# Softmax sums in a two-layer attention kernel: reciprocals of six of eight heads (or pairs of heads) go through DRAM instead of through TensorE

## The chip, the cores and the metric

The kernel runs on one core of a Trainium2 chip. The metric is the device time of one execution in microseconds (us). The core has a matrix engine (TensorE, PE in the profile), three engines for elementwise work (VectorE as DVE, ScalarE as ACT, GpSimd as POOL), and SyncE (SP), which in this kernel does nothing but issue transfers (DMAs). Each engine works through its own list of instructions in order; an instruction that waits holds up everything behind it on that engine. Data on the chip lies in 128 partitions; PSUM holds eight banks for the results of matmuls.

## The reference

A two-layer encoder on 512 frames of 1024 features. Layer one is multi-head latent attention with 8 heads of 128 values; layer two is chunked attention with a learned bias and 16 heads of 64 values. Each is followed by a SwiGLU feed-forward block, and each sub-layer has a norm before and after it. What the change touches is the softmax, the same in both layers:

```python
s = jnp.where(mask[None, None], s, -jnp.inf)
p = jax.nn.softmax(s, axis=-1).astype(v.dtype)
return jnp.einsum('bhqk,bkhd->bqhd', p, v)
```

The kernel computes exp(s) first, multiplies it by the values, and divides by the sum of the exponentials afterwards.

## The kernel before

All activations lie transposed: features on the partitions, the 512 frames along the row. To keep float32 precision with fast matmuls, each operand is split into a high and a low part (`split`, L143: ACT casts to the high part, DVE subtracts it to get the low part), and a product is three matmuls (`mm3`, L354 to L356), or two where one operand is already stacked.

`attention` (L511) runs both attention layers. Time is cut into slots: slot i computes the scores of head i // 4 for the 128 queries of block i % 4. In `scores` (L486) PE writes the scores into a bank of the kind "s" (two of them), DVE adds the mask or bias and finds the extreme value (L492), and ACT takes exp and sums each row into `sums` (L494). Two slots later `turn` (L498) transposes the exponentials on PE into a bank of the kind "t" (two of them, L506), and ACT and DVE split them. When the four blocks of a head are done, its `pv` multiplies by the values: in layer one inside `start_a`, in layer two inside `start_b` (L1502, L1503). `pv` also takes the reciprocals of the sums (L995, L1511) and returns a function `rest` that scales the head's output and splits it into `oh` and `ol`, the operands of the output projection. In between, `weave` puts in matmuls of a filler: the projections that make the queries and keys of later heads (`fill_a`, `fill_b`), and the first half of the output projection.

The sums come out with one query per partition, but the outputs have queries along the row. So the reciprocals have to be turned and spread over all partitions. Before, PE does it. In layer one `spread` (L463) broadcasts each of four columns to 128x128 and transposes it into a "t" bank called `bc` (L467, four PE instructions per head). In layer two two heads share 128 partitions, so the work is done once per pair: ACT writes the eight columns out to a 128x512 tile `rw` (L1514, two copies), and PE transposes that in four pieces into a "t" bank called `rs` (L1523). DVE then multiplies `of`, the output, by that bank (L1000, L1524).

Transfers on SP's list around this work: weight tiles `raw` (L285), the rows of the rotary queries `qr` of layer one (L894), and in layer two the queries and keys of each pair (L1477, twelve transfers per pair, from tiles `fh` and `f`) and one `bias` tile per head (L1454).

A scheduler places the instructions of each engine by its own estimate of when operands are ready and by the order in which the code issues them. So the place of a row on an engine follows from the code only roughly.

Of the kernel before, what the change touches and what calls it, by code (L numbers as in the profile page):

```python
# [10 lines left out]
F32 = mybir.dt.float32  # L11
# [19 lines left out]
NQT = S // P  # L31
# [37 lines left out]
def trunk(ctx: ExitStack, tc: tile.TileContext, a, out):  # L69
# [25 lines left out]
    def small(name="sm"):  # L95
        return sp.tile([P, 4], F32, tag="small", name=name_(name))
# [54 lines left out]
    class Pair:  # L151
# [4 lines left out]
        def __init__(self, src):  # L156
            self.src, self.raw = src, {}
# [313 lines left out]
    def spread_sb(col):  # L471
# [2 lines left out]
        nc.scalar.copy(o, b)  # L474
        return o


    class Head:

        def __init__(self, qk, bt, scale, pv, sums):
            self.qk, self.bt, self.scale, self.pv, self.sums = qk, bt, scale, pv, sums
            self.p, self.pt = {}, None

        def scores(self, qt):  # L486
# [24 lines left out]
    def attention(n_heads, start, fill, first, units, after):  # L511
# [33 lines left out]
        if late:  # L545
            late.pop()()


    class Post:
# [424 lines left out]
    def start_a(h):  # L974
        fill.until(h)
        qh, ql, kh, kl = qk_a.pop(h)
        r = qr.pop(h)

        def qk(o, qt, n):
            q_ = slice(qt * P, (qt + 1) * P)  # L980
            nc.tensor.matmul(o, qh[:, q_], kh[:, :n], start=True, stop=False)
            nc.tensor.matmul(o, qh[:, q_], kl[:, :n], start=False, stop=False)
            nc.tensor.matmul(o, ql[:, q_], kh[:, :n], start=False, stop=False)
            nc.tensor.matmul(o, r[:, q_], kr1[:, :n], start=False, stop=False)
            nc.tensor.matmul(o, r[:, q_], kr2[:, :n], start=False, stop=True)

        def pv(pth, ptl):
            fill.until("v")
            o = bank()
            v_ = slice(h * VD, (h + 1) * VD)  # L990
            for kt in range(NQT):
                q_ = slice(kt * P, S)
                mm3(o[:, q_], (va[kt][:, 0, v_], va[kt][:, 1, v_]), (pth[:, kt, q_], ptl[:, kt, q_]),
                    kt == 0, kt == NQT - 1)
            V.reciprocal(sums, sums)  # L995
            of = U(name="of")
            nc.scalar.copy(of, o)

            def rest():
                V.tensor_tensor(of, of, spread(sums), op=OP.mult)  # L1000
# [7 lines left out]
        return Head(qk, lambda n: mask[:, S - n:], lambda qt: nsq[:, qt:qt + 1], pv, sums)  # L1008

    firsts = []  # L1010
    fill = Filler(fill_a())
    attention(H_A, start_a, fill, 13, 8 + 5 * 7 + 6 + 14, False)
    fill.drain()
    st.close()

# [466 lines left out]
    def start_b(h):  # L1482
# [14 lines left out]
        def pv(pth, ptl):  # L1497
# [11 lines left out]
            V.tensor_tensor(of[(LO, HI)[e]], o[:64], t[:64], op=OP.add)  # L1509
            if e:  # L1510
                V.reciprocal(sums[pr], sums[pr])  # L1511
                rw = U(name="rw")
                for j in range(2):
                    nc.scalar.copy(rw.rearrange("p (i e d) -> p i e d", e=2, d=HD)[:, :, j],  # L1514
                                   sums[pr][:, j].unsqueeze(2).to_broadcast([P, NQT, HD]))

            def rest():
                if e == 0:
                    return
                r = bank("t", "rs")  # L1520
                for i in range(NQT):
                    i_ = slice(i * P, (i + 1) * P)
                    nc.tensor.transpose(r[:, i_], rw[:, i_], ident)  # L1523
# [7 lines left out]
        return Head(qk, lambda n: bt[:, :n][:, ::-1], lambda qt: -1.0, pv, sums[pr][:, e])  # L1531

    bias(0)
    firsts = []
# [13 lines left out]
    for tt in range(NQT):  # L1548
        v_split(b[tt], 1, tt)

    attention(H_B, start_b, fill, 12, 7 * 16 + 14, True)
    fill.drain()
    st.close()

# [89 lines left out]
```

## Time and profile before

| what | us |
|---|---|
| median of 3 runs (lowest to highest) | 1136.78 (1135.42 to 1137.72) |
| the profiled execution | 1136.21 |
| its span in the trace | 1134.4 |
| start and projections, 0 to 60 | 60 |
| attention of layer one, 60 to 165 | 105, PE busy 104.27, DVE 70.58, ACT 62.35 |
| feed-forward of layer one, 165 to 490 | 325, PE busy 321.27, DVE 291.58 |
| shared values, first queries and keys, 490 to 596 | 106, PE busy 104.54 |
| attention of layer two, 596 to 757 | 161, PE busy 158.40, DVE 118.57, ACT 105.35 |
| the rest of layer two, 757 to 1134.4 | 377.4, PE busy 364.72 |

Times inside the trace count from the start of the span. A busy share of PE says less than it seems: matmuls are pipelined, so one that is recorded as 272 ns long lets the next one start after about 110 ns. "Loading weights" on PE (PEld) is the step that puts the stationary operand in place; a wait of PE shows there first.

### The profile page before, as it was taken

What the parts mean: (1) busy time and instruction counts of PE and PEld (TensorE: products, weight loads), DVE (VectorE), ACT (ScalarE), POOL (GpSimd) and SP (SyncE); (2) the same over time, 40 slices, a digit from 0 to 9 for tenths busy, and PEclk for the clock granted to TensorE, in tenths of its full rate; (3) what the DMA queues carried; (4) which work ended last, traced back from release to release, by engine and by line L of the source; (5) the groups of instructions that cost most, each with busy time, mean ns of one, the idle gap of its engine ahead of it and who ended that gap; (6) DMA issues with size and microseconds to landing.
All of it is one profiled execution on the core that took longest, in us unless ns stands there. A gap on an engine that the chain in (4) does not pass through costs nothing.

```text
span 1134.4 us, 18987 instructions
## 1 busy us (share of the span) xinstructions
PE 1109.6 (98%) x6973; PEld 984.5 (87%) x6973; DVE 935.2 (82%) x1675; ACT 682.6 (60%) x1335; POOL 65.1 (6%) x90
## 2 busy tenths in 40 slices
PE   8999999999999999999999999999999999999996
PEld 6888889999999998787888888779999999997785
DVE  7787738999899889879758887648999899889867
ACT  6476637655555556578437766656755555567574
POOL 1200000100000002400000000001000000003300
PEclk9999999999999999999999999999999999999998
DMA  7433125423323349932456656634323422359902
GB/s 234 113 106 94 56 91 188 140 85 93 119 87 97 136 149 261 213 102 70 165 147 167 158 161 154 160 106 170 135 75 93 131 94 100 116 180 260 201 1 75
DMA packets 62414, 149.80 MB, mean 132 GB/s; under 512 B 8368, under 2 KB 10160, under 8 KB 62320
## 3 DMA queue, kind: packets, MB, share of 16 engines
q1 hardware_dynamic: 55840, 137.00, 38.5%
q0 software_dynamic: 6336, 11.54, 6.0%
q8 instruction: 55, 0.90, 0.3%
q14 instruction: 39, 0.32, 0.1%
q10 hardware_dynamic: 144, 0.04, 0.0%
HBM read 119.52 MB, written 8.59 MB: 113 GB/s over the span
## 4 chain that ended last, share of the span: by engine, by line
PE 85%; DVE 7%; ACT 3%; DMA 2%; issue 2%; POOL 1%; SPq 0%; DVEq 0%; POOLq 0%; ACTq 0%
PE al L1378 16%; PE b L354 11%; PE b L355 10%; PE b L356 10%; PE be L1378 8%; PE al L1171 8%; PE ga L1378 4%; PE be L1171 4%; PE de L1171 3%; PE ga L1171 3%; PE pt L506 2%; DVE wlo L145 2%; DMA raw<-in_w_pair 1%; ACT whi L144 1%; PE b L1502 1%
## 5 line engine op out<-in xcount | busy, mean ns | idle before, releaser
L144 ACT CAST whi<-raw 128x1024 fp32r<-128x1024 f32 (+3 forms) x224 | 225.6, 1007 | 213.9 <-PE al L1378 73.1
L145 DVE TENSOR_TENSOR wlo<-raw,whi 128x1024 fp32r<-128x1024 f32 (+3 forms) x224 | 261.0, 1167 | 67.4 <-ACT whi L144 64.9
L1378 PE MATMUL al<-th,whi 128*128 128x256 f32 x432 | 123.2, 285 | 1.8 <-DVE ut L1390 1.8
L1378 PE MATMUL al<-th,wlo 128*128 128x256 f32 x432 | 121.2, 281 | 0.0
L1378 PE MATMUL al<-tl,whi 128*128 128x256 f32 x432 | 121.2, 281 | 0.0
L354 PE MATMUL b<-xh,whi 128*128 128x512 f32 (+1 forms) x304 | 115.7, 383 | 1.8 <-ACT xh L148 1.8
L355 PE MATMUL b<-xl,whi 128*128 128x512 f32 (+1 forms) x304 | 112.9, 371 | 0.0
L356 PE MATMUL b<-xh,wlo 128*128 128x512 f32 (+1 forms) x304 | 112.8, 371 | 0.0
L174 DVE TENSOR_TENSOR raw<-raw,raw 128x1024 f32<-128x1024 f32 x72 | 86.8, 1220 | 3.3 <-DMA raw<-in_w_pair 3.1
L1378 PEld LDWEIGHTS al<-th,whi 128*128 128x128 f32 x432 | 81.4, 188 | 4.1 <-DVE ut L1390 2.2
L1378 PEld LDWEIGHTS al<-th,wlo 128*128 128x128 f32 x432 | 81.4, 188 | 0.0
L1378 PEld LDWEIGHTS al<-tl,whi 128*128 128x128 f32 x432 | 81.4, 188 | 0.0
L494 ACT ACTIVATE p<-p,mn 128x128 f32<-128x128 f32 (+1 forms) x96 | 53.9, 562 | 31.7 <-DVE mn L492 31.5
L145 DVE TENSOR_TENSOR ptl<-pt,pth 128x128 fp32r<-128x128 f32 (+1 forms) x96 | 46.2, 486 | 28.8 <-ACT pth L144 23.2
L354 PEld LDWEIGHTS b<-xh,whi 128*128 128x128 f32 x304 | 57.3, 189 | 9.6 <-ACT xh L148 2.7
L356 PEld LDWEIGHTS b<-xh,wlo 128*128 128x128 f32 x304 | 57.4, 189 | 8.8
L144 ACT CAST whi<-wd 128x512 fp32r<-128x512 f32 x86 | 49.8, 620 | 24.2 <-PE de L1171 8.7
L355 PEld LDWEIGHTS b<-xl,whi 128*128 128x128 f32 x304 | 57.5, 189 | 7.2 <-DVE xl L149 0.5
L145 DVE TENSOR_TENSOR wlo<-wd,whi 128x512 fp32r<-128x512 f32 x86 | 56.4, 686 | 7.6 <-ACT whi L144 7.2
L144 ACT CAST pth<-pt 128x128 fp32r<-128x128 f32 (+1 forms) x96 | 40.3, 424 | 28.6 <-PE pt L506 27.9
L1171 PE MATMUL al<-whi,ph 128*128 128x512 f32 x132 | 51.6, 391 | 0.0
L1171 PE MATMUL al<-whi,pl 128*128 128x512 f32 x132 | 51.6, 391 | 0.0
(304 smaller groups left out, 3260.7 us busy)
## 6 DMA issues: line engine op xcount, KB each, us to landing
raw<-in_w_pair SPq DMA_DIRECT2D x72, 512.0 KB, 3.6
wd<-in_w_down SPq DMA_DIRECT2D x54, 256.0 KB, 5.6
raw<-in_w_o SPq DMA_DIRECT2D x16, 512.0 KB, 3.5
raw<-in_w_gu SPq DMA_DIRECT2D x16, 512.0 KB, 3.8
raw<-in_w_down SPq DMA_DIRECT2D x16, 512.0 KB, 4.5
raw<-in_w_qkb SPq DMA_DIRECT2D x16, 512.0 KB, 3.5
wd<-in_w_down POOLq DMA_DIRECT2D x22, 256.0 KB, 5.4
wd<-raw POOLq DMA_DIRECT2D x22, 256.0 KB, 5.3
```

Source lines behind the costliest of these rows:

```text
L144: return (nc.scalar.copy(dst_hi, src), V.tensor_tensor(dst_lo, src, dst_hi.bitcast(F32), op=OP.subtract))
L145: V.tensor_tensor(dst_lo, src, dst_hi.bitcast(F32), op=OP.subtract))
L174: V.tensor_tensor(t, x, y, op=OP.add)
L354: nc.tensor.matmul(o, l[0], r[0], start=start, stop=False)
L355: nc.tensor.matmul(o, l[0], r[1], start=False, stop=False)
L356: nc.tensor.matmul(o, l[1], r[0], start=False, stop=stop)
L494: nc.scalar.activation(p[:, :n], p[:, :n], AF.Exp, bias=mn[:, :1], scale=-1.0, accum_out=self.sums[:, qt:qt + 1])
L506: nc.tensor.transpose(t[:, kt * P:(kt + 1) * P], p[:, kt * P:(kt + 1) * P], ident)
L1171: nc.tensor.matmul(to[e], l[c], r[d], start=j < 4 and k == 0 and n == 0, stop=k == NF // 2 - 1 and n == 2, skip_group_check=True)
L1378: nc.tensor.matmul(o, l[c], r[d], start=first_ and n == 0, stop=k == K2 - 1 and n == 2, skip_group_check=True)
L1502: nc.tensor.matmul(o[:, q_], vv, pth[:, kt, q_], start=kt == 0, stop=False)
```

## The change

For the first six of the eight heads of layer one, and the first six of the eight pairs of layer two, the reciprocals no longer pass through PE. A new function `spread_far` writes them to a small DRAM tensor `sums` in the order of the queries (one transfer per head, so two for a pair; the 128x4 tile goes out as 512 separate elements of four bytes), and reads that row of 2 KB back once for every partition into a tile `bc` of 128x512 (one transfer of 256 KB for a head of layer one, two of 128 KB for a pair). All of them are issued by SP; the reading transfer waits until the writing one has landed. The multiplication on DVE then reads `bc` instead of a PSUM bank. `attention` no longer runs `rest` at the next slot (layer one) or in the same group of slots (layer two), but four slots after `pv` for the far heads and one slot after for the last two (`near`), which keep the way through PE.

```diff
+    def spread_far(sums, n, to):
+        row = a["sums"][to]
+        for e in range(n):
+            v = sums[:, e] if n > 1 else sums
+            nc.sync.dma_start(row[e].rearrange("(t p) -> p t", p=P), v)
+        o = U(name="bc")
+        w = P // n
+        for e in range(n):
+            nc.sync.dma_start(o[e * w:e * w + w], bass.AP(tensor=row.tensor, offset=row[e].offset, ap=[[0, w], [1, S]]))
+        return o
...
@@ attention
-            if late and not after:
-                late.pop()()
             if i >= 6 and i % NQT == 2:
                 t = heads.pop((i - 6) // NQT)
-                late.append(t.pv(*t.pt))
+                rest = t.pv(*t.pt)
+                late.append((i + (1 if t.near else NQT), rest))
             if 2 <= i < slots + 2:
                 t, qt = divmod(i - 2, NQT)
                 heads[t].turn(qt)
-            if late and i % NQT == 3:
-                late.pop()()
+            while late and i >= late[0][0]:
+                late.pop(0)[1]()
...
@@ pv of layer one
+            far = None if near else spread_far(sums, 1, h)
 
             def rest():
-                V.tensor_tensor(of, of, spread(sums), op=OP.mult)
+                V.tensor_tensor(of, of, spread(sums) if near else far, op=OP.mult)
...
-        sums = small("sums")
+        sums, near = small("sums"), h >= H_A - 2
...
@@ pv of layer two
             if e:
                 V.reciprocal(sums[pr], sums[pr])
-                rw = U(name="rw")
-                for j in range(2):
+                rw = U(name="rw") if near else spread_far(sums[pr], 2, H_A + pr)
+                for j in range(2 if near else 0):
                     nc.scalar.copy(rw.rearrange("p (i e d) -> p i e d", e=2, d=HD)[:, :, j],
                                    sums[pr][:, j].unsqueeze(2).to_broadcast([P, NQT, HD]))
 
             def rest():
                 if e == 0:
                     return
-                r = bank("t", "rs")
-                for i in range(NQT):
+                r = bank("t", "rs") if near else rw
+                for i in range(NQT if near else 0):
                     i_ = slice(i * P, (i + 1) * P)
                     nc.tensor.transpose(r[:, i_], rw[:, i_], ident)
                 V.tensor_tensor(of, of, r, op=OP.mult)
...
+        near = pr >= H_B // 2 - 2
...
+    aps["sums"] = nc.dram_tensor("sums", (H_A + H_B // 2, 2, S), F32, kind="Internal").ap()
```

What this does to the lists of three engines is shown at three places. In the rows of the changed kernel the line numbers are its own: L354 to L356 and L145 are unmoved, L506 has become L519, L492 L505, L1494 L1507, L1495 L1508, L1477 L1490, L1454 L1467, and L1000 L1013.

First PE in layer two, at the scaling of the second pair; `sc` are scores, `pt` the transposed exponentials, `b` a projection of the filler. Before:

```order
L506 MATMUL pt_7248<-ident,p_7182 128x128 x2
L354 MATMUL b_7175<-xh_6122,whi_7099 128x512
L355 MATMUL b_7175<-xl_6123,whi_7099 128x512
L356 MATMUL b_7175<-xh_6122,wlo_7100 128x512
L1494 MATMUL sc_7269<-k_2_6796,q_2_6795 128x128
L1523 MATMUL rs_7253<-ident,rw_7219 128x128 x4
L1495 MATMUL sc_7269<-k_2_6797,q_2_6795 128x128
```

The same place in the changed kernel:

```order
L519 MATMUL pt_7235<-ident,p_7167 128x128 x2
L354 MATMUL b_7160<-xh_6110,whi_7079 128x512
L355 MATMUL b_7160<-xl_6111,whi_7079 128x512
L356 MATMUL b_7160<-xh_6110,wlo_7080 128x512
L1507 MATMUL sc_7246<-k_2_6784,q_2_6783 128x128
L1508 MATMUL sc_7246<-k_2_6785,q_2_6783 128x128
```

The four transposes into `rs` are gone and nothing has come in their place on PE; that is so at all twelve places.

Second SP in layer two, from the bias tile after the keys of pair 2 to the first keys of pair 3. Before:

```order
L1454 DMA bias_7266<-in_rel 128x512
L1477 DMA q_3_7056<-fh_7167 64x512 x2
L1477 DMA q_3_7056<-f_7166 64x512 x2
L285 DMA raw_7758<-in_w_qkb 128x1024
L1454 DMA bias_7376<-in_rel 128x512
L1477 DMA k_3_7057<-fh_7296 64x512 x2
```

In the changed kernel:

```order
L1467 DMA bias_7243<-in_rel 128x512
L483 DMA sums<-sums_6917 128x4x1 x2
L1490 DMA q_3_7036<-fh_7152 64x512
L1490 DMA q_3_7036<-f_7151 64x512
L1490 DMA q_3_7036<-fh_7152 64x512
L1490 DMA q_3_7036<-f_7151 64x512
L285 DMA raw_7729<-in_w_qkb 128x1024
L487 DMA bc_7206<-sums 64x512 x2
L1467 DMA bias_7358<-in_rel 128x512
L1490 DMA k_3_7037<-fh_7273 64x512 x2
```

The two writes of pair 1 stand ahead of the queries of pair 3, the two reads ahead of the next bias tile and of the keys of pair 3.

Third DVE in layer one, where the second half of the rotary queries has just been made and the scores of head 3's last block (128x512) and of head 4's first (128x128) are handled; `ql` and `kl` are the low parts of queries and keys of heads 4 and 5. Before:

```order
L492 ISA p_1238,mn_1239<-sc_1232,mask,nsq 128x512
L492 ISA mn_1239 128x1
L145 TENSOR_TENSOR ol_1252<-of_1214,oh_1251 128x512
L145 TENSOR_TENSOR ptl_1217<-pt_1255,pth_1216 128x2x128
L995 RECIPROCAL sums_1099<-sums_1099 128x4
L145 TENSOR_TENSOR ptl_1217<-pt_1277,pth_1216 128x3x128
L145 TENSOR_TENSOR ql_1223<-b_1157,qh_1222 128x512
L145 TENSOR_TENSOR ptl_1217<-pt_1305,pth_1216 128x4x128
L145 TENSOR_TENSOR kl_1225<-b_1228,kh_1224 128x512
L145 TENSOR_TENSOR wlo_1533<-raw_1296,whi_1532 128x1024
L145 TENSOR_TENSOR ql_1313<-b_1273,qh_1312 128x512
L492 ISA p_1269,mn_1270<-sc_1263,mask,nsq 128x128
```

In the changed kernel:

```order
L145 TENSOR_TENSOR ptl_1211<-pt_1266,pth_1210 128x3x128
L145 TENSOR_TENSOR wlo_1518<-raw_1285,whi_1517 128x1024
L145 TENSOR_TENSOR ql_1222<-b_1148,qh_1221 128x512
L145 TENSOR_TENSOR kl_1224<-b_1227,kh_1223 128x512
L145 TENSOR_TENSOR ql_1302<-b_1262,qh_1301 128x512
L145 TENSOR_TENSOR kl_1304<-b_1307,kh_1303 128x512
L145 TENSOR_TENSOR ol_1218<-of_1053,oh_1217 128x512
L505 ISA p_1237,mn_1238<-sc_1231,mask,nsq 128x512
L505 ISA mn_1238 128x1
L505 ISA p_1258,mn_1259<-sc_1252,mask,nsq 128x128
L505 ISA mn_1259 128x1
L1013 TENSOR_TENSOR of_1205<-of_1205,bc_1208 128x512
```

The last scores of head 3, which stood ahead of the low parts of the queries and keys, now stand behind all four of them. Behind the scores follows the scaling of head 2, whose tile `bc` SP reads only after the sixteen `qr` transfers.

More of the change, by code (lines that the diff above doesn't have):

```diff
@@ L509, in turn, with attention @@
             split(self.pt[0][:, :qt + 1, q_], self.pt[1][:, :qt + 1, q_], tv)
-    def attention(n_heads, start, fill, first, units, after):
+    def attention(n_heads, start, fill, first, units):
         slots = n_heads * NQT
@@ L541, in attention @@
                 heads[t].turn(qt)
[L542 to L543 removed]
+            while late and i >= late[0][0]:
+                late.pop(0)[1]()
             weave(first + rate * (i + 1))
[L545 to L546 removed]
+        while late:
+            late.pop(0)[1]()
     class Post:
@@ L1005, in pv @@
             return rest
-        sums = small("sums")
-        return Head(qk, lambda n: mask[:, S - n:], lambda qt: nsq[:, qt:qt + 1], pv, sums)
+        sums, near = small("sums"), h >= H_A - 2
+        return Head(qk, lambda n: mask[:, S - n:], lambda qt: nsq[:, qt:qt + 1], pv, sums, near)
     firsts = []
     fill = Filler(fill_a())
-    attention(H_A, start_a, fill, 13, 8 + 5 * 7 + 6 + 14, False)
+    attention(H_A, start_a, fill, 13, 8 + 5 * 7 + 6 + 14)
     fill.drain()
@@ L1529, in pv @@
             return rest
-        return Head(qk, lambda n: bt[:, :n][:, ::-1], lambda qt: -1.0, pv, sums[pr][:, e])
+        near = pr >= H_B // 2 - 2
+        return Head(qk, lambda n: bt[:, :n][:, ::-1], lambda qt: -1.0, pv, sums[pr][:, e], near)
     bias(0)
@@ L1549, in trunk @@
         v_split(b[tt], 1, tt)
-    attention(H_B, start_b, fill, 12, 7 * 16 + 14, True)
+    attention(H_B, start_b, fill, 12, 7 * 16 + 14)
     fill.drain()
```

4 lines of the change are left out of this document (2 added, 2 removed).

## The prediction

> **What bounds the kernel now.** I read the page first: busy times, the slices, and the chain of work that ended last.
>
> ```profile
> span 1134.4 us, 18987 instructions
> PE 1109.6 (98%) x6973; PEld 984.5 (87%) x6973; DVE 935.2 (82%) x1675; ACT 682.6 (60%) x1335; POOL 65.1 (6%) x90
> PE   8999999999999999999999999999999999999996
> PE 85%; DVE 7%; ACT 3%; DMA 2%; issue 2%; POOL 1%; SPq 0%; DVEq 0%; POOLq 0%; ACTq 0%
> ```
>
> PE is busy nearly everywhere and makes up 85% of the chain; transfers make up 2%. So an instruction taken from PE should shorten the time, as long as PE really is what the stage waits for. The change touches the two attention stages only, so I read those in stretches of 20 us (columns: length, then busy us and instructions of PE, PEld, DVE, ACT, POOL, PE clock, DMA share, GB/s).
>
> ```profile
> 80.00:100.00 20.00, 19.77 (x116) 17.01 (x116) 14.91 (x35) 10.97 (x29) 0.00 (x0) 1.00 0.10 34
> 100.00:120.00 20.00, 19.64 (x118) 16.78 (x117) 16.27 (x41) 14.72 (x37) 0.00 (x0) 1.00 0.43 126
> 620.00:640.00 20.00, 19.89 (x113) 16.52 (x112) 18.38 (x43) 14.89 (x38) 0.29 (x2) 1.00 0.63 165
> 640.00:660.00 20.00, 19.87 (x113) 16.62 (x112) 18.20 (x44) 14.82 (x38) 0.29 (x2) 1.00 0.63 154
> 720.00:740.00 20.00, 18.85 (x97) 14.18 (x96) 14.22 (x37) 13.04 (x33) 0.00 (x0) 1.00 0.52 131
> ```
>
> In layer one DVE has 4 to 5 us of 20 free, in layer two at first under 2. PE bounds both, but in layer two DVE is close behind, and towards its end (720 to 740) PE itself waits 1.2 us of 20.
>
> **What PE is relieved of.** The chain, in order of time (start, length, what), shows what a group of four transposes holds up:
>
> ```profile
> 81.39 0.44 PE bc L467 x4
> 134.80 0.44 PE bc L467 x4
> 638.57 0.66 PE rs L1523 x4
> 715.82 0.44 PE rs L1523 x4
> ```
>
> One transpose is recorded as 274 ns (row below), but four take 0.44 us of the chain, since they overlap; the 0.66 counts the last one to its end. Twelve groups go: 12 x 0.44 = **5.3 us**. With them go waits. The groups by line (busy us, mean ns, then idle before and its releasers):
>
> ```profile
> L467 PE MATMUL bc<-ident,sums 128*128 128x128 f32 x32 | 4.8, 274 | 0.0
> L1523 PEld LDWEIGHTS rs<-ident,rw 128*128 128x128 f32 x32 | 3.4, 141 | 3.0 <-ACT rw L1514 1.5 <-issue 0.6 <-DVE ptl L145 0.5
> ```
>
> In layer one PE did not wait ahead of `bc`. In layer two its weight loading waited 3.0 us ahead of eight `rs` groups, 2.3 us for six. What stands behind them on PE are transposes of exponentials, which wait for the same ACT and the same "t" banks, so part of that wait will only move. Between 0 and 2.3 I take the middle, **1.1 us**.
>
> The other removed and changed instructions:
>
> ```profile
> L1514 ACT COPY rw<-sums x16: 390/402/406, 619.7 to 757.1; 128x256 f32<-128x256 f32 x16
> L1000 DVE TENSOR_TENSOR of<-of,bc x8: 675/682/689, 81.9 to 165.1; 128x512 f32<-128x512 f32 x8
> L145 DVE TENSOR_TENSOR ol<-of,oh 128x512 fp32r<-128x512 f32 x8 | 5.5, 690 | 1.4 <-ACT oh L144 1.3
> ```
>
> Twelve copies of 0.40 us leave ACT, which has 5 us of 20 free: no gain beyond the wait just counted. The multiplication reads SBUF in place of PSUM: `of<-of,bc` from PSUM takes 682 ns, `ol<-of,oh` from SBUF 690, so nothing changes on DVE.
>
> **What SP gets.** Per layer-one head one write and one read, per pair two and two. No transfer of this trace moves 512 pieces of four bytes. The nearest rows (KB each, median us to landing; then the timeline of SP and the issue times in ns):
>
> ```profile
> rot<-sincos SPq DMA_DIRECT2D x4, 48.0 KB, 1.7
> inv<-in_inv_freq SPq DMA_DIRECT2D x1, 0.5 KB, 2.7
> bias<-in_rel SPq DMA_DIRECT2D x16, 256.0 KB, 3.3
> k<-fh SPq DMA_DIRECT2D x32, 128.0 KB, 2.4
> 34.63 1.76 SPq L818 DMA_DIRECT2D rot<-sincos  x4
> L1477 SPq DMA_DIRECT2D k<-fh x32: 461/591/603, 569.6 to 730.0; - x32
> L1454 SPq DMA_DIRECT2D bias<-in_rel x16: 328/334/529, 503.1 to 714.1; - x16
> ```
>
> A small write to DRAM (`rot`) lands after 1.7 us. `inv` is 128 pieces of four bytes, a read, and lands after 2.7; if all of that grew with the number of pieces, 512 would take 10.8. So a write lands between 1.7 and 10.8 us; I take 2.7, the row with the same kind of piece (with 1.7 fixed and 1.0 for each 128 pieces it would be 5.7). The reads are the size of `bias` (3.3) and `k` (2.4). Issuing takes 1.76 / 4 = 0.44 us each, as `rot` does; 64 rows of `k` take longer than 128 of `bias`, so issue time does not follow the number of pieces.
>
> Can SP hold that in layer two? The reciprocals of pairs 1 and 2, and SP's transfers between them:
>
> ```profile
> 632.41 0.18 DVE L1511 RECIPROCAL sums<-sums 128x8 f32<-128x8 f32 x1
> 633.54 1.10 SPq L1477 DMA_DIRECT2D q<-fh  x2
> 638.34 0.33 SPq L1454 DMA_DIRECT2D bias<-in_rel  x1
> 644.08 1.11 SPq L1477 DMA_DIRECT2D k<-fh  x2
> 648.74 0.20 DVE L1511 RECIPROCAL sums<-sums 128x8 f32<-128x8 f32 x1 [0.55 <-ACT p L494]
> ```
>
> A pair lasts 16.3 us. SP is busy for 12 x 0.59 with queries and keys, and about 1.4 with two bias and two weight tiles (0.33 each, up to 0.4 with gaps): 8.5 us. Four new issues make 1.8, and 6.0 are left for waiting. The writes go out at about 632.7 and 633.1, ahead of q, which then is done at about 636.2; the second has landed at 636.2 by my value, so the reads go out at 636.7 and 637.1, and land by 640.4 even at 3.3. Behind the waiting read stand the bias tile, which SP issued at 638.34, and the keys at 644.08: neither is late. The multiplication stands some twenty instructions behind the reciprocal on DVE's list, which is nearly full there, so it comes after about 643. So for most pairs the new waits cost nothing; where a write stands behind eight key transfers (8 x 0.6 = 4.8 us, pairs 3 and 5) it may be late. I put 0 in the sum and keep 0 to 2 us.
>
> **A place that gets worse.** In layer one around 100 us the lists are rearranged (third place in the change). The timeline there, before:
>
> ```profile
> 102.62 0.48 DVE L492 CUSTOM_DVE_ANT_0 p<-sc,mask,nsq 128x256 f32<-128x256 f32 x1
> 104.64 0.75 DVE L492 CUSTOM_DVE_ANT_0 p<-sc,mask,nsq 128x512 f32<-128x512 f32 x1 [0.19 <-PE sc L985]
> 107.64 1.22 SPq L894 DMA_DIRECT2D qr<-rl  x2
> 108.44 0.39 PE L356 MATMUL b<-ckh,wlo 128*128 128x512 f32 x1
> 109.72 1.23 DVE L145 TENSOR_TENSOR wlo<-raw,whi 128x1024 fp32r<-128x1024 f32 x1 [0.34 <-ACT whi L144]
> 110.75 0.28 PE L985 MATMUL sc<-kr,qr 128*128 128x256 f32 x1
> ```
>
> Before, the 128x512 scores left their bank at 105.4 (104.64 + 0.75), and PE ended head 4's 128x256 scores at 111.0 with five products of head 3's values and one transpose group done besides, about 1.5 us of work (three of 512 columns at 0.23, two of 384 at 0.17, a group of 0.44). Now the 128x512 row waits for the last `kl`. The keys leave PE at about 108.0 (they did at 108.8), their cast on ACT ends near 108.6, `kl`, `ol` and the 128x512 scores follow on DVE at 0.6 to 0.7 us each: 110.5. Only then has PE a bank for 128x256, which ends at 111.1; PE stood idle for some 2 us. So at 111 PE is 1.6 us behind the old kernel, where the first term has it 1.3 us ahead (three groups have gone by then). The place costs 2.9 us; if the 0.9 us gained by the first two groups carries through it, **2.1 us**, which I take, between 0 (all made up in later waits) and 3. The read for head 2 stands behind the `qr` transfers, which end at 108.9: it lands at 108.9 + 0.4 + 3.3 = 112.6, and DVE is there at about 111. PE would feel that wait at the same scores, so it lies inside these bounds.
>
> **Sum.** -5.3 - 1.1 + 2.1 = -4.3 us. Against the profiled execution's own 1136.2 us that gives **1131.9 us**. The median of the three runs is 0.6 us above it, so 1131.9 to 1132.5 is the same forecast.
>
> **A rule that speaks against the change.** The row `inv` gave 2.7 us for 128 pieces of four bytes. The Trainium skill, "DMA: Bandwidth & Descriptors", section "Rules for kernel authors", says that a transfer whose last dimension is not contiguous becomes one descriptor per element and should be rearranged. The same page's specifications say that below 512 bytes the DMA reads, modifies and writes. No run here shows what 512 such writes to DRAM take; by that rule the write would lie towards the far end of my range, and the sum would be that of the second rival.
>
> **Rivals.**
> 1. *DVE takes over as the pace.* From 620 to 660 it is busy 18.38 and 18.20 of 20 us. If half of PE's relief in layer two turns into waiting for DVE (6 x 0.44 / 2 = 1.3 us gained, no wait saved), and the place near 100 us costs 3, against 2.6 gained in layer one, the total is -0.9: **1135.3**, no measurable change. Against it: PE bounds the longer part of both stages.
> 2. *The small writes land late.* SP cannot pass the read that waits. From the budget above, each us beyond 6.0 (plus 0.4 of a weight tile issued meanwhile) delays a pair's keys by one. At a landing of 8 us that is 1.6 x 6 = 9.6 us in layer two, so -4.3 + 9.6 = +5.3: **1141.5**, slower; at 10.8 it is 4.4 x 6 = 26, 1158. It decides from about 7.1 us of landing. For it: 512 pieces, two such writes at once, and DMA shares of 0.5 to 0.6. Against it: 2.7 for 128 pieces includes a fixed part, as 1.7 for `rot` shows, and the 5.7 worked out with it stays under 7.1.
> 3. *More is freed.* If all 2.3 us of waits go and the place near 100 us costs nothing, it is -5.3 - 2.3 = -7.6: **1128.6**.
>
> That the change would not do what it says is excluded by the lists: 48 transposes are off PE, none came back.
>
> **How the numbers follow.** Forecast 0.55, rival one 0.22, rival two 0.11, rival three 0.12. A change of 0.2% (2.3 us, so below 1134.5 or above 1139.1) is about what measurement can tell from none. Faster: 0.55 + 0.12, less 0.04 for the forecast with all its unknown costs at the bad end = 0.63. Same: 0.22 + 0.04 = 0.26. Slower: 0.11. The range goes from 1128.4, just past rival three, to 1137.0, past rival one with the 2 us of late reads; it leaves out rival two and little else.
>
> **What would show it.** In the trace after: 8 transposes each of `bc<-ident,sums` and `rs` left of 32, and the chain without those groups up to the last two heads. Right for the SP part: `sums` landing in about 2.7 us, no wait of PE for `bc`, `q` or `k`. Right for the bad place: PE idle ahead of the 128x256 scores near 108 us, ended by DVE. Wrong: `sums` landing over 6 us with keys late behind it (rival two), or attention stages as long as before with new waits of PE on L505 and L519's casts in layer two (rival one).

## The result and the profile after

| | us |
|---|---|
| before, median of 6 runs (lowest to highest) | 1136.59 (1134.52 to 1137.72) |
| after, median of 6 runs | 1231.15 (1229.14 to 1236.61) |
| ratio, 95% interval | 1.0848 (1.0833 to 1.0864) |
| the profiled execution after, its span | 1236.61, 1234.8 |

The change makes the kernel 8.5% slower, some 95 us. The forecast was 1131.9, between 1128.4 and 1137.0. From the page of the changed kernel: busy times, the slices of PE and of PE's granted clock, and the chain by engine:

```profile
span 1234.8 us, 18944 instructions
PE 1134.7 (92%) x6925; PEld 1000.8 (81%) x6925; DVE 934.8 (76%) x1675; ACT 679.1 (55%) x1323; POOL 64.8 (5%) x90
PE   9987779999999999999998756779999999999996
PEclk9998689999999999999999877889999999999999
PE 71%; DMA 17%; DVE 6%; ACT 2%; issue 2%; SPq 2%; POOL 1%; DVEq 0%; POOLq 0%; ACTq 0%
```

PE now has two holes, one in each attention stage, and its busy time rises from 1109.6 to 1134.7 us although 48 instructions are gone. Transfers, 2% of the chain before, are 17%. The chain through layer one says which:

```profile
74.20 8.74 DMA sums<-sums
82.99 4.99 DMA bc<-sums
88.81 9.84 DMA sums<-sums
98.67 5.02 DMA bc<-sums
...
108.49 11.40 DMA qr<-rh
```

A write, its read, the next head's write, its read: the stage runs at the pace of the round trip. Then a transfer of rotary rows, normally 2.0 us, takes 11.4. The transfers by size and median time to landing:

```profile
raw<-in_w_o SPq DMA_DIRECT2D x16, 512.0 KB, 10.1
bias<-in_rel SPq DMA_DIRECT2D x16, 256.0 KB, 6.6
q<-fh SPq DMA_DIRECT2D x16, 128.0 KB, 11.8
bc<-sums SPq DMA_DIRECT2D x6, 256.0 KB, 5.8
bc<-sums SPq DMA_DIRECT2D x12, 128.0 KB, 6.4
sums<-sums SPq DMA_DIRECT2D x18, 2.0 KB, 10.7
```

The writes land after 10.7 us, and some of what was there before is late too: `bias` took 3.3 before, `raw<-in_w_o` 3.5, `q<-fh` 2.3. Who waits, first on SP's list, then on the engines (us in total, times, longest):

```profile
SPq L487 <- DMA sums<-sums: 73.7, 12, 10.2
```

```profile
DVE of L1013 <- DMA bc<-sums: 32.8, 6, 6.8
DVE raw L304 <- DMA raw<-in_w_qkb: 28.7, 6, 12.2
DVE of L1537 <- DMA bc<-sums: 26.9, 3, 12.5
PEld b L1516 <- DVE ptl L145: 20.1, 3, 12.4
```

SP stands 74 us behind the writes. DVE waits 60 us for `bc`, and 29 for weights that have nothing to do with the change (8.8 before); PE's longest waits are DVE's, passed on. In stretches (columns as in the prediction):

```profile
90.00:100.00 10.00, 10.00 (x52) 8.69 (x51) 4.87 (x12) 4.73 (x13) 0.00 (x0) 0.88 0.92 24
...
120.00:140.00 20.00, 13.88 (x55) 11.20 (x56) 9.53 (x23) 7.09 (x19) 0.00 (x0) 0.66 0.32 93
```

From 90 to 100 us the DMA engines count as 92% busy and move 24 GB/s. The packet records say what fills them: the 46 packets of 4 KB that start between 90.2 and 98 us take 3.2 us in the median, where 0.16 is the median of such packets over both attention stages. From 120 to 140 PE is busy 13.9 of 20 us, at a mean clock of 0.66. From the start of layer one's attention to the end of layer two's, the granted clock is 0.50 for 99 us, and PE is busy in 62 of them; in the kernel before it is 1.00 there throughout. So, as an estimate, half of those 62, or 31 of the 95 us lost, are not waits of PE but its work at half rate.

Two marks split the loss by stage for all runs below: the first write of `mid` stands behind the attention of layer one, and the attention of layer two lies between the first `keep` and the last `mid`. Before, then after:

```profile
L1055 SPq DMA_DIRECT2D mid<-x x16: 319/320/427, 201.8 to 801.8; - x16
L1442 SPq DMA_DIRECT2D keep<-x x8: 320/418/995, 539.9 to 545.1; - x8
```

```profile
L1068 SPq DMA_DIRECT2D mid<-x x16: 319/323/834, 242.7 to 903.7; - x16
L1455 SPq DMA_DIRECT2D keep<-x x8: 319/397/446, 581.0 to 586.2; - x8
```

Layer one is 242.7 - 201.8 = 40.9 us later; layer two takes 903.7 - 581.0 = 322.7 instead of 801.8 - 539.9 = 261.9, 60.8 more. Of the runs below, one execution of e2_free_read ran at a mean granted clock of 0.59 and took 1712.83 us; its ratio leaves it out, and the marks are from a second run.

### The profile page after: what moved, and what is told of

Same layout as the page of the kernel before. It is cut to its first block, busy times and chain, and to the rows that moved or that the text cites. A ratio compares the mean times of both kernels' runs of the same rounds, so it can differ in the third digit from the quotient of the medians.

```text
span 1234.8 us, 18944 instructions
## 1 busy us (share of the span) xinstructions
PE 1134.7 (92%) x6925; PEld 1000.8 (81%) x6925; DVE 934.8 (76%) x1675; ACT 679.1 (55%) x1323; POOL 64.8 (5%) x90
## 4 chain that ended last, share of the span: by engine, by line
PE 71%; DMA 17%; DVE 6%; ACT 2%; issue 2%; SPq 2%; POOL 1%; DVEq 0%; POOLq 0%; ACTq 0%
PE al L1391 15%; PE b L354 8%; PE b L355 8%; PE be L1391 8%; PE b L356 8%; DMA sums<-sums 7%; PE al L1184 7%; PE ga L1391 4%; PE be L1184 4%; DMA bc<-sums 3%; PE de L1184 2%; PE ga L1184 2%; DMA raw<-in_w_qkb 2%; DVE wlo L145 1%; DMA k<-f 1%
## 5 line engine op out<-in xcount | busy, mean ns | idle before, releaser
L145 DVE TENSOR_TENSOR wlo<-raw,whi 128x1024 fp32r<-128x1024 f32 (+3 forms) x224 | 260.7, 1165 | 79.4 <-ACT whi L144 78.4
L354 PE MATMUL b<-xh,whi 128*128 128x512 f32 (+1 forms) x304 | 119.5, 396 | 0.2 <-ACT xh L148 0.2
L355 PE MATMUL b<-xl,whi 128*128 128x512 f32 (+1 forms) x304 | 115.4, 380 | 0.0
L356 PE MATMUL b<-xh,wlo 128*128 128x512 f32 (+1 forms) x304 | 114.6, 377 | 0.0
L145 DVE TENSOR_TENSOR ptl<-pt,pth 128x128 fp32r<-128x128 f32 (+1 forms) x96 | 46.2, 485 | 41.0 <-ACT pth L144 33.4
L356 PEld LDWEIGHTS b<-xh,wlo 128*128 128x128 f32 x304 | 59.1, 195 | 9.7
L354 PEld LDWEIGHTS b<-xh,whi 128*128 128x128 f32 x304 | 59.5, 196 | 8.6 <-ACT xh L148 1.3
L145 DVE TENSOR_TENSOR wlo<-wd,whi 128x512 fp32r<-128x512 f32 x86 | 56.2, 685 | 7.3 <-ACT whi L144 7.0
L519 PE MATMUL pt<-ident,p 128*128 128x128 f32 x240 | 46.3, 294 | 13.0 <-DVE ptl L145 12.1
```

The lines of the kernel that those rows point to most:

```text
L145: V.tensor_tensor(dst_lo, src, dst_hi.bitcast(F32), op=OP.subtract))
L354: nc.tensor.matmul(o, l[0], r[0], start=start, stop=False)
L355: nc.tensor.matmul(o, l[0], r[1], start=False, stop=False)
L356: nc.tensor.matmul(o, l[1], r[0], start=False, stop=stop)
L519: nc.tensor.transpose(t[:, kt * P:(kt + 1) * P], p[:, kt * P:(kt + 1) * P], ident)
```

## The experiments

All against the kernel before in the same batch. "One" and "two" are the shifts of the two marks in each run's trace; the execution traced lies above the median in some, by 4.5 us in e8_one_transpose and 6.9 in e10_two_16b_pool.

| run | what differs | median us | ratio (interval) | one | two |
|---|---|---|---|---|---|
| after | the change | 1231.15 | 1.0848 (1.0833 to 1.0864) | +40.9 | +60.8 |
| e1_16b | pieces of 16 bytes | 1141.4 | 1.0063 (1.0042 to 1.0084) | +3.4 | +3.0 |
| e2_free_read | read waits for no write | 1204.34 | 1.061 (1.0592 to 1.0628) | +29.5 | +41.2 |
| e3_no_write | no write at all | 1134.17 | 0.9999 (0.999 to 1.0008) | +6.3 | -5.3 |
| e4_write_only | before, plus writes | 1175.02 | 1.0357 (1.0324 to 1.039) | +0.9 | +42.0 |
| e5_write_actq | the same from ACT's queue | 1174.36 | 1.0363 (1.0338 to 1.0389) | -0.1 | +38.1 |
| e6_two_only_no_write | e3, layer two alone | 1128.31 | 0.995 (0.9937 to 0.9963) | +0.5 | -5.9 |
| e8_one_transpose | one transpose, rows of 512 bytes, layer two | 1140.39 | 1.0063 (1.0043 to 1.0083) | +0.2 | +5.5 |
| e9_two_16b | 16 bytes, strided multiplication, layer two | 1162.61 | 1.0229 (1.021 to 1.0248) | +0.5 | +26.1 |
| e10_two_16b_pool | e9, reads from GpSimd | 1141.39 | 1.0059 (1.0037 to 1.008) | +0.1 | +6.4 |
| e15_mm_bank | e8, another bank | 1143.72 | 1.009 (1.0067 to 1.0112) | +0.6 | +9.1 |
| e16_mm_bank_late | e15, nominally later | 1151.96 | 1.0161 (1.0118 to 1.0203) | -0.3 | +16.7 |
| e17_mm_bank_pool | e15, all from GpSimd | 1146.56 | 1.0101 (1.0076 to 1.0126) | +0.8 | +9.1 |

The marks of e2_free_read are from e2b_free_read. Two more runs, e12_forms and e14_spacing, were timed once each and follow below.

**Is it the pieces, or the round trip?** Theory A is that the write in small pieces is late, B that any round trip is, C that the rearranged lists cost the time.

```diff
-            nc.sync.dma_start(row[e].rearrange("(t p) -> p t", p=P), v)
+            nc.sync.dma_start(row[e].rearrange("(p t) -> p t", p=P), v)
```

> The reciprocals are written in the order in which they lie in the tile (128 pieces of 16 bytes instead of 512 of 4 bytes), so they come back in another order and the outputs of the far heads are scaled by wrong values; all instructions of PE, DVE, ACT and their order stay as in the changed kernel. Theory A (the number of pieces makes the write late): the write lands in about 2.5 to 4 us instead of 10.7, SP's waits ahead of the reads shrink by the same 7 us each, and most of the loss goes: 1130 to 1150 us. Theory B (a round trip through DRAM is late by itself, however many pieces): landing stays near 10 us and the time near 1231. Theory C (later scaling and the rearranged lists cost the time, not the transfers): time stays above 1200 though the write lands early.

```profile
bc<-sums SPq DMA_DIRECT2D x6, 256.0 KB, 3.7
bc<-sums SPq DMA_DIRECT2D x12, 128.0 KB, 4.8
sums<-sums SPq DMA_DIRECT2D x18, 2.0 KB, 1.9
```

The write lands in 1.9 us instead of 10.7, and 90 of the 97 us lost against this batch's 1134.23 are gone, with every list of PE, DVE and ACT as in the changed kernel. So B and C together, less what PE is relieved of, come to about 7 us.

**Is it the wait for the write, or what the write does to others?** In e2_free_read the write stays and the read comes from elsewhere; in e3_no_write the write is gone too; e4_write_only is the kernel before with the writes added.

```diff
-bass.AP(tensor=row.tensor, offset=row[e].offset, ap=[[0, w], [1, S]])
+bass.AP(tensor=a["rel"].tensor, offset=a["rel"].offset + to * a["rel"].shape[1], ap=[[0, w], [1, S]])
```

> The write of 512 pieces is kept, but the tile bc is read from a row of the bias table in DRAM, so the read waits for no write, and the far heads are scaled by the values of that row. Theory A1 (the loss is the chain write, then read, then multiplication, with SP standing between): the read can go out at once, lands in about 3 to 6 us, and the time falls to 1135 to 1150 us. Theory A2 (the loss is that the 512 pieces occupy the queues, so that everything behind them is late): reads, bias tiles and weights still land in 5 to 12 us, and most of the loss stays, over 1180 us. Theory C (order and later scaling): near 1231.

> The same kernel as e2_free_read (512-piece writes, reads from the bias table that wait for no write), for a trace at an undisturbed clock. With the time at about 1204 us, the losses should stand in late transfers: if the pieces occupy the queue, reads and bias tiles issued within some 10 us behind a write land over 6 us after their issue, and those issued elsewhere at 2.4 to 4 us as in the run without writes.

```diff
-            nc.sync.dma_start(row[e].rearrange("(t p) -> p t", p=P), v)
+            pass
```

> As the run before it, with no write at all: the reads from the bias table alone, the far heads scaled by its values. If the transposes taken from PE are worth what was forecast and the reads are hidden, 1130 to 1134 us. If the time is still over 1150 us, the reads (256 KB each) or the order of the lists carry a part of the loss themselves. Theory C again near 1231.

```diff
+            if h < H_A - 2:
+                write_far(sums, 1, h)
...
+                if pr < H_B // 2 - 2:
+                    write_far(sums[pr], 2, H_A + pr)
```

> The kernel before with its way through PE kept, and the eighteen writes of 512 pieces added that nobody waits for. Theory A1 (only the wait for the write costs): within 0.5% of the kernel before, 1135 to 1142 us. Theory A2 (the pieces hold up other transfers): bias tiles, queries and keys land several us later than before (3.3 and 2.4 us), and the time goes over 1160 us.

Freed of its write, the read saves only 27 us. Of the 97 us, 70 stay with nothing waiting for the writes. In the trace of e2b_free_read the reads and `q`, which wait for no write, still land late:

```profile
q<-fh SPq DMA_DIRECT2D x16, 128.0 KB, 12.1
...
bc<-in_rel SPq DMA_DIRECT2D x12, 128.0 KB, 12.1
```

The writes alone cost 41 us, all in layer two. Its chain shows how; two writes left SP at 617.8 and 618.4:

```profile
619.00 12.33 DMA raw<-in_w_qkb
...
648.68 11.96 DMA raw<-in_w_qkb
...
678.10 8.79 DMA q<-f
```

The weights behind the writes take 12.3 us (3.5 before); in layer two DVE waits for such weights 23.7 us in all, and PE for DVE. In layer one the same writes cost 0.9 us: the only wait of an engine for a transfer there is one of 1.3 us, for a row of `qr`. So A2 holds: the harm goes mostly through other transfers. The `bc` tile of layer one is such a transfer as well: in e2b_free_read DVE waits 25.2 us for it, and layer one loses 29.5 us, of which e3_no_write has 6.3 without any write.

**Is it SP's queue?**

```diff
-            nc.sync.dma_start(row[e].rearrange("(t p) -> p t", p=P), v)
+            nc.scalar.dma_start(row[e].rearrange("(t p) -> p t", p=P), v)
```

> As e4_write_only (the kernel before, plus eighteen 512-piece writes that nobody waits for), but the writes are issued by ACT, into its own queue, instead of by SP. Theory A2a (the transfers behind a write wait because they stand in the same queue): bias, queries, keys and weights land at 2.3 to 3.6 us again, and the time falls from 1175 to 1136 to 1145 us. Theory A2b (the pieces occupy the DMA engines that all queues share): the transfers stay late at 4 to 12 us and the time stays above 1160 us.

```profile
616.37 8.93 DMA raw<-in_w_qkb
...
682.05 8.02 DMA k<-f
```

No: with the writes in ACT's queue, SP's weights and keys still take 8.9 and 8.0 us here, and the time is the same. What is held up is not one queue alone. Some of the 38 us in layer two may be of another kind: one exp on ACT waited 8.4 us for a write to land, which no engine did in e4_write_only.

**Why is such a write slow?** I had put it down to the number of pieces. Two runs measure that by itself, with writes nobody waits for.

```diff
+        if form == 0:
+            nc.sync.dma_start(row[:P].rearrange("(t p) -> p t", p=P), sums[:, :1])
...
+        elif form == 2:
+            nc.sync.dma_start(row[:S].rearrange("(t p) -> p t", p=P), sums)
...
+        elif form == 4:
+            nc.sync.dma_start(row[:4 * S].rearrange("(t p x) -> p t x", p=P, x=4), sums.unsqueeze(1).to_broadcast([P, 4, 4]))
```

> The disputed cost by itself: the kernel before, its way through PE kept, plus one write per far head or pair that nobody waits for, each of six forms used once in layer one and once in layer two: 128, 256 and 512 pieces of 4 bytes, and 128, 256 and 512 pieces of 16 bytes. Theory A-count (a write costs by its number of pieces, whatever their size): 128 pieces land in about 2 to 3 us in both sizes, 256 in 4 to 6, 512 in 9 to 11, also at 16 bytes. Theory A-size (pieces of 4 bytes are the trouble): 512 pieces of 16 bytes land in 2 to 4 us, and 128 pieces of 4 bytes take no less than 2.7. The time, with far fewer pieces than the eighteen writes of e4_write_only, 1140 to 1155 us.

By KB each: 0.5 and 1.0 are 128 and 256 pieces of 4 bytes, 4.0 and 8.0 are 256 and 512 of 16. Below it the 512 pieces of 4 bytes, by their own line (least, median, most):

```profile
scr<-sums SPq DMA_DIRECT2D x2, 0.5 KB, 7.5
scr<-sums SPq DMA_DIRECT2D x2, 1.0 KB, 8.6
scr<-sums SPq DMA_DIRECT2D x2, 8.0 KB, 3.4
scr<-sums SPq DMA_DIRECT2D x2, 4.0 KB, 2.8
```

```profile
L486 SPq DMA_DIRECT2D scr<-sums x2: 370/451/532, 93.3 to 708.6; - x2
...
DMA to landing us min/median/max: 7.6/7.7/7.9
```

My count theory falls on both sides: 128 pieces of 4 bytes take 7.5 us, as long as 512, and 512 pieces of 16 bytes take 3.4. The time, 1136.51 in one execution, was below the 1140 to 1155 expected. Transfers were held up here too: the weights `raw<-in_w_o` issued at 689.66 and 709.22, right behind two 4-byte writes of layer two, landed after 11.3 and 10.8 us, but no engine waited for them. Left were the size of a piece, or its neighbours: in the change, the sixteen elements in 64 bytes of DRAM come from sixteen partitions.

```diff
+        x = {0: 16, 1: 128, 2: 16, 3: 2, 4: 1, 5: 4}[form]
+        d = row[:S * x].rearrange("(t p x) -> p t x", p=P, x=x)
+        if form == 0:
+            nc.sync.dma_start(d[:, :, 0], sums)
...
+        elif form == 2:
+            nc.sync.dma_start(d[:, :1, 0], sums[:, :1])
```

> Like e12_forms, with other forms, each once in layer one and once in layer two, that nobody waits for: 512 pieces of 4 bytes whose places in DRAM lie 64 bytes apart, 512 bytes apart and 16 bytes apart; 128 pieces of 4 bytes 64 bytes apart; 512 pieces of 8 bytes side by side; and, as the control, 512 pieces of 4 bytes side by side, as in the changed kernel. Theory G (many engines write to the same short stretch of DRAM at once): pieces 64 or 512 bytes apart land in 2 to 4 us, 16 bytes apart in 3 to 4, 8 bytes side by side in 4 to 6, the control in 7 to 8. Theory A-size (a piece of 4 bytes is slow wherever it goes): all forms of 4 bytes land in 6.9 to 9.5 us as in e12_forms, 8 bytes lie between.

First 128 pieces of 4 bytes 64 bytes apart (0.5 KB) and 512 of 8 bytes side by side (4.0 KB); then 512 of 4 bytes, 16 bytes apart, by their line:

```profile
scr<-sums SPq DMA_DIRECT2D x2, 0.5 KB, 1.4
scr<-sums SPq DMA_DIRECT2D x2, 4.0 KB, 3.9
```

```profile
L494 SPq DMA_DIRECT2D scr<-sums x2: 377/380/383, 126.6 to 660.5; - x2
...
DMA to landing us min/median/max: 3.4/3.4/3.4
```

The same 128 pieces of 4 bytes land in 1.4 us when they lie 64 bytes apart, and in 7.5 side by side. Each of these rows holds one landing of two, and the other forms have none, since the trace lacks a few records. The semaphore updates (sixteen per transfer) fill this in: 2.0 us for the second write of 128 pieces, 5.4 for the second of 8 bytes, 3.3 for the other 16 bytes apart; 3.3 and 2.2 us for 512 pieces 64 bytes apart, 1.8 and 3.1 for 512 bytes apart, 8.1 and at least 9.1 for the control. So neither the count nor the size of the pieces makes the write slow, but how close together they start in DRAM: 4 bytes apart it took 6.9 to 9.5 us, 8 bytes apart 3.9 and 5.4, from 16 bytes on 1.4 to 3.5. That fits theory G. Its reason, that many engines write to one short stretch at once, is not shown: in every form neighbouring pieces came from different partitions, and no run let them come from one.

The one execution of e14_spacing took 1146.62 us, 11.5 above its batch, and its second mark is 10.9 later: the weights behind the pieces of 8 bytes and behind those 16 bytes apart landed after 6.5 us, those behind the control after 8.7. So a single write with weights behind it is enough, and in part even one that lands early itself.

The packet records of the changed kernel fit: the pieces of the write issued at 88.81 leave within 0.4 us (89.72 to 90.09, 7 to 9 ns each), and the landing comes 8.6 us after the last of them.

**What was the relief worth, and where?** By e3_no_write the whole change without its write gains nothing: layer one loses 6.3 us, layer two gains 5.3. Layer one's loss, in its windows and PE's timeline:

```profile
108.00:110.00 2.00, 0.33 (x1) 0.19 (x1) 1.64 (x2) 2.00 (x5) 0.00 (x0) 1.00 0.44 101
...
112.00:114.00 2.00, 0.69 (x3) 0.69 (x4) 1.52 (x5) 0.71 (x2) 0.00 (x0) 0.50 1.02 350
114.00:116.00 2.00, 2.00 (x11) 1.90 (x10) 1.27 (x4) 1.09 (x6) 0.00 (x0) 0.50 0.77 305
116.00:118.00 2.00, 2.00 (x8) 1.77 (x7) 0.77 (x3) 0.95 (x3) 0.00 (x0) 0.50 0.04 14
```

```profile
109.35 0.33 PE L993 MATMUL sc<-kh,qh 128*128 128x128 f32 x1 [1.88 <-ACT kh L144]
110.84 0.33 PE L994 MATMUL sc<-kl,qh 128*128 128x128 f32 x1 [1.16 <-DVE kl L145]
...
113.31 0.58 PE L993 MATMUL sc<-kh,qh 128*128 128x256 f32 x1 [1.80 <-DVE mn L505]
```

It is the place that the prediction named, but PE waits 1.88 + 1.16 + 1.80 = 4.8 us there, and then has half its clock to 118.4, with 5.1 us of work in that time: another 2.6 us lost. Less the 2.6 us that the prediction gave the six groups of layer one, that makes 4.8 of the 6.3; the rest is not placed. If so, layer two alone should be faster than before:

```diff
-        sums, near = small("sums"), h >= H_A - 2
+        sums, near = small("sums"), True
```

> As e3_no_write, but layer one scales its heads as before, through PE; layer two reads its tiles from the bias table without any write, so the far pairs are scaled by the values of that table. Theory D (in e3_no_write layer two gained 5.3 us and layer one lost 6 around 100 us, where PE stood idle for the keys and its clock fell to half): 1128 to 1130.5 us, and no stretch under full clock near 110 us. Theory E (what is taken from PE is given back anywhere, since another engine paces): within 0.2% of the kernel before, 1132 to 1136 us.

It is: 0.995, 5.7 us, with no slow clock near 110 us. The relief of PE is real where the lists do not get worse.

**Can that be had with a real round trip?** Not in any form that ran. In e8_one_transpose PE transposes the reciprocals once, so that rows of 512 bytes can be written:

```diff
+        nc.tensor.transpose(t[:8, :P], sums.rearrange("p a b -> p (a b)"), ident)
+        c = U(name="ct")
+        nc.scalar.copy(c[:8, :P], t[:8, :P])
+        nc.sync.dma_start(row.rearrange("e (t p) -> (e t) p", p=P), c[:8, :P])
```

> Layer one as before. In layer two, for the first six pairs, one PE transpose of the 128x8 reciprocals and one ACT copy of 8x128 make eight rows of 512 bytes, which one transfer writes to DRAM; the two reads back are as in the changed kernel. By theory A (pieces make the write late) the write lands in about 2 us, no transfer behind it is late, and three quarters of the relief of layer two is kept: 1129 to 1133 us, faster than both kernels. By theory B (the round trip through DRAM costs by itself): no better than e1_16b, 1137 us or more.

It took 1140.39 us, on the side of theory B, although SP waits for the six writes only 7.8 us in all.

In e9_two_16b the pieces are of 16 bytes and DVE picks the order; in e10_two_16b_pool GpSimd issues the reads:

```diff
+            nc.sync.dma_start(row.rearrange("e (p t) -> p e t", t=NQT), sums)
...
+            V.tensor_tensor(of.rearrange("f (t p) -> f t p", p=P), of.rearrange("f (t p) -> f t p", p=P),
+                            r.rearrange("f (p t) -> f t p", t=NQT), op=OP.mult)
```

> Layer one as before. Layer two writes the reciprocals of a far pair in the order of the tile, 256 pieces of 16 bytes in one transfer, reads them back with one transfer, and the multiplication on DVE reads bc with a stride of four elements, so that the result is the reference's. Theory A: the write lands in 2 to 5 us, SP waits some 2 us a pair, nothing else is late, and the layer-two gain of the run without writes (5.3 to 5.9 us) is mostly kept: 1128 to 1133 us. Theory F (the relief shows only where DVE need not wait for a real round trip; with the order that the scheduler makes for a late tile, layer two loses, as it did in e8_one_transpose, by 5.5 us against the kernel before): 1136 to 1142 us.

> As e9_two_16b, but the two reads of a pair are issued by GpSimd, so that SP never waits for a write to land. If SP's wait is what e9_two_16b loses, it is faster than that by 1 to 5 us; if the order of the lists is, no different by over 2 us; if GpSimd itself stands behind a bias tile, slower.

e9_two_16b took 1162.61 us, far above either of its figures. Its groups and waits:

```profile
L1536 DVE TENSOR_TENSOR of<-of,bc x6: 1061/1064/1087, 630.7 to 749.8; 128x512 f32<-128x512 f32 x6
```

```profile
DVE of L1536 <- DMA bc<-sums: 22.9, 6, 5.2
```

The strided multiplication takes 1064 ns instead of 687, and DVE waits for every tile. With the reads on GpSimd, in two halves, e10_two_16b_pool is 21 us faster, not the 1 to 5 expected, and DVE's waits for `bc` fall to 9.0 us. The traces show a second difference between the two: the single read of 128x512 lands 8.8 to 10.5 us after its issue and gives three semaphore updates, two of them late, while each half gives sixteen and lands after 3.8 to 7.4, or 2.9 where SP issues it (e15_mm_bank). So the form of the single read has a share in that wait; how much SP's list added was not told apart. Three runs then went after the rest: the transpose in another bank, the scaling eight slots later, and write and reads on GpSimd.

```diff
-        t = bank("t", "rt")
+        t = bank(name="rt")
```

> As e8_one_transpose, but the one transpose of the reciprocals goes into one of the four banks of the projections instead of one of the two t banks, which it held there until ACT's copy came (2.6 us for the first pair, about 8 for the sixth). Theory H (holding that bank is what e8_one_transpose lost in layer two): 1128 to 1133 us, faster than the kernel before. Theory F (the order made for a late tile, or the round trip, loses it): 1137 to 1143 us again.

```diff
-                late.append((i + (1 if t.near else NQT), rest))
+                late.append((i + (1 if t.near else 2 * NQT), rest))
```

> As e15_mm_bank, with the scaling eight slots after the values instead of four, so that DVE has at least 10 us between the landing and the multiplication. If the wait of DVE for bc still costs, 1 to 4 us faster than e15_mm_bank; if the order of the lists decides, no trend: anywhere within 6 us of it.

```diff
-        nc.sync.dma_start(row.rearrange("e (t p) -> (e t) p", p=P), c[:8, :P])
+        nc.gpsimd.dma_start(row.rearrange("e (t p) -> (e t) p", p=P), c[:8, :P])
```

> As e15_mm_bank, but the write and the two reads of a pair are issued by GpSimd, whose list in layer two holds only the bias masks. In e15_mm_bank the last chain ran through SP: it waited 8.2 us in all for the six writes to land and 12 us for the copies before them, and queries and keys of the next pair, which stand behind, were late (PE waited 1.9 us for a key at 630.9). If SP's list is what is left of the loss, SP shows no such waits, no engine waits for keys, and the time is 1128 to 1134 us, no slower than the kernel before. If the order of the lists on PE, DVE and ACT is, it stays at 1138 us or more, with late keys gone.

The bank was not it (1143.72). In e15_mm_bank SP waits for the writes, and PE once for a key. In e17_mm_bank_pool SP's wait is gone, but PE still waits for a key at the same place, and DVE now waits for `bc`. SP and PE of the one, PE and DVE of the other:

```profile
SPq L489 <- DMA sums<-ct: 8.2, 6, 2.3
```

```profile
630.93 0.30 PE L1509 MATMUL sc<-k,q 128*128 128x128 f32 x1 [1.91 <-DMA k<-fh]
```

```profile
631.27 0.30 PE L1509 MATMUL sc<-k,q 128*128 128x128 f32 x1 [1.55 <-DMA k<-f]
```

```profile
DVE of L1539 <- DMA bc<-sums: 9.6, 5, 3.1
```

So SP's wait for the write was not what made the key late. The waits change places, and the time stays at 1.009 to 1.010. Asking for a later scaling does not help: the scheduler leaves the multiplication 19 to 27 instructions behind its reciprocal on DVE in e15_mm_bank and e16_mm_bank_late alike, and the latter is 8 us slower, outside both of its expectations, with more waits of PE for the scores. How much of the 15 us between e6_two_only_no_write and e15_mm_bank is the round trip and how much the order of the lists stays open; about 140 instructions of PE, 50 of DVE and 35 of ACT stand at other places in the lists of the two.

## Why the prediction was wrong

**The write's landing, 2.7 us: wrong, and the step that failed.** The prediction took "2.7, the row with the same kind of piece". The write took 10.7. The row `inv` is a read into SBUF; it tells nothing of 512 neighbouring elements of DRAM written from 128 partitions. The far end of the range, 10.8, was nearly right by accident: it multiplied by the number of pieces, and in e12_forms 128, 256 and 512 pieces of 4 bytes took 7.5, 8.6 and 7.7 us. The rule of the Trainium skill, "DMA: Bandwidth & Descriptors", section "Rules for kernel authors", pointed to the right side. But one piece per element is not slow by itself: 512 pieces of 4 bytes land in 3.4 us when they start 16 bytes apart (e14_spacing). Nor is 512 bytes, below which the same page of the Trainium skill has the DMA read, modify and write, a border for the landing here: pieces of 16 bytes landed in 1.9 us (e1_16b).

**Rival two was the right mechanism for a quarter of the loss.** The prediction gave it a chance of 0.11. It priced SP's list in layer two only, 26 us at 10.8, and so came to 1158 even with the right landing. Waiting for the write, in both layers, is worth 27 us (after against e2_free_read). What had no term: the writes hold up transfers that do not depend on them, 41 us with nothing waiting for the writes (e4_write_only). Nor had the clock a term: PE's work at half rate, about 31 us in the trace of the changed kernel.

**"For most pairs the new waits cost nothing": wrong with the landing, and in layer one too.** There the prediction checked only the one read behind the `qr` transfers. It did not compare write and read with the distance between one head's reciprocal and the next, ahead of which the multiplication stands: 8 to 13 us for the far heads in the trace before. At its own values, 2.7 + 3.3, a round trip fits; at 10.7 + 5.8 it fits nowhere, and the chain above shows write, read, write, read.

**The transposes, -5.3, and their waits, -1.1: right in kind.** For layer two they make -2.6 - 1.1 = -3.7; measured without the write, with the later scaling and its lists: -5.7 (1134.17 times 0.005; 4.2 to 7.1 by the interval), a little more than forecast.

**The place near 100 us, +2.1: right place, too small.** With the six groups saved there, the forecast for layer one was -2.6 + 2.1 = -0.5; e3_no_write has +6.3. PE's waits there were 4.8 us, where the prediction had PE idle for some 2 and a cost of 2.9 in all, and the slow clock behind them was in no term. With this size alone the change would have been no gain: e3_no_write is at 0.9999.

**Rivals one and three** do not decide: DVE's pace did not take the relief in e6_two_only_no_write. The upper end of the range, 1137.0, was meant to hold rival one with 2 us of late reads; that sum is 1137.3.

## What to carry to other kernels

Before small results go to DRAM and back, look at how close together its pieces start in DRAM: here rows of 16 bytes from one partition, or single elements 16 bytes apart, landed within 1.4 to 3.5 us, and elements side by side after 7 and more. Price a slow transfer not only by who waits for it but by what is issued behind it, in another engine's queue too. And waits of PE of some 5 us in a row cost more than their length, where the clock is low afterwards as it was here.

## What was not expected of the hardware

- A write of 128 to 512 pieces of 4 bytes, side by side in DRAM and from different partitions, lands after 6.9 to 9.5 us (e12_forms), and after 9.2 to 11.7 in the changed kernel; 128 such pieces 64 bytes apart after 1.4 and 2.0, 512 pieces 16 bytes apart after 3.3 and 3.4.
- Weights issued 0.6 us behind two such writes took 12.3 us instead of 3.5; with the writes in another engine's queue still 8.9. Behind a single write of 256 pieces of 4 bytes they took 11.3 (e12_forms).
- In e3_no_write PE was mostly idle from 107.5 to 113.3 us, and the granted clock was 0.50 from 111.6 to 118.4. The Trainium skill, "TensorE: Matmul & The Clock Gate", section "Part 1: The HAM clock gate (the "warmup" mystery)", tells of a clock gate that is set by how busy PE has been of late, and lists two states, a full and a half rate; the trace agrees: its clock records hold 1.00 and 0.50 only.
- A multiplication on DVE that reads one operand with a stride of four elements took 1064 ns instead of 687.
